# A two-block transformer kernel: the mixer's opening loads and products reordered, and the linear attention written in three tied steps per head and direction

## The chip, the core and the metric

The kernel runs on one core of one Trainium2 chip. The metric is the device time of one execution in microseconds (us). TensorE (PE) multiplies, VectorE (DVE) and ScalarE (ACT) work on tiles, GpSimd (POOL) helps, and SP issues most DMA transfers. SBUF is the memory on the core, PSUM the one into which TensorE writes.

## The reference

A first block (a mixer, then 32 experts of which four are used per token) is followed by a second block of two layers. The change lies in the mixer: it normalises 256 tokens `x` and 256 context tokens, modulates them, projects them with one wide `w_in`, runs a gated delta rule (8 heads) and a gated linear attention (GLA, 4 heads), each in both directions over context and tokens, and merges the branches.

```python
mod_lat = split(silu(c) @ w_mod + b_mod, 6); mod_ctx = split(silu(c_ctx) @ w_mod + b_mod, 6)
h_lat = rms_norm(x, norm_mix_g) * (1 + sc1) + sh1
h_ctx = rms_norm(ctx, norm_mix_g) * (1 + csc1) + csh1
p_lat, p_ctx = h_lat @ w_in, h_ctx @ w_in
# delta rule on silu(conv(q, k, v)), then the linear attention, per direction:
log_a = log_sigmoid(lr @ gla_gate_w + gla_gate_b) / 16
def step(s, xs):                       # chunks of the sequence
    intra, qg, kd, v, gl = xs          # qg = q exp(gcum), kd = k exp(gcum[-1] - gcum)
    o = intra + qg @ s                 # intra = tril((q e^(gcum-ref)) (k e^(ref-gcum))^T) v
    s = s * gl[:, None] + kd.T @ v
    return s, o
y = sigmoid(g_a) * (rms_norm(o_a) * silu(z) @ w_out_a) + sigmoid(g_b) * (rms_norm(o_b) * silu(r) @ w_out_b)
x = x + g1 * (y @ w_out)
x = x + g2 * moe_ffn(modulate(rms_norm(x)))    # 32 experts, top 4
out = second_block(x)
```

## The kernel before, in words

The program is recorded engine by engine with a tile layer: a scheduler sorts the instructions of each engine by the priority in which they were written and by its model of the engines; tiles come from pools with a tag and a number of buffers, and the layer adds the waits. So the order on an engine is not that of the code; it is shown below where it matters. Products of full accuracy are made of three: a weight `w` is split into a high part `wh` (a cast by ScalarE, line 150) and a low part `wl` (a subtraction by VectorE, line 151), and `mm3` (line 164) adds `wh`xhigh, `wh`xlow and `wl`xhigh, 24 products for the 8 rows of 128 of the inner dimension. `proj_fm` and `proj_tm` are the two forms of a projection: `proj_fm` loads 128 columns of a weight with `load_w` (line 172), splits them with `parts`, and multiplies.

`phase1` is the mixer. Its opening (lines 257 to 335) loads `x` into `xin`, eight 1 MB pieces of `w_mod` (line 250) and, between the third and the fourth, the context; then the small weights `wsm` (the gates' columns) and constants: `cum` (into `resB`), `adt` (decay rates), `cw` (convolution), `gw` (GLA gates) and a mask. `mod_mm` (line 255) multiplies a piece by the two conditioning columns `cT`. Each pair of token tiles, `x` first, is squared and scaled (lines 301 to 306), transposed on TensorE (line 311) and copied to `xT` (line 313). The modulation rows are evacuated (line 316) and transposed into columns `mc` and `G1` (lines 319 to 324). Then, for each of 8 blocks `kk`, ScalarE writes the modulated block rounded, `hTh` (line 329, two halves of 256), VectorE writes it in full, `hf` (line 331, two halves), and subtracts: `hTl` (line 333). The first products on these are the gating one, `psm` (24 products with `wsh` and `wsl`), and the first projection (columns 4640), with which the gating product shares the tag of its PSUM tile; projections of columns 1024 and 1152 follow for the convolutions, which VectorE does.

`DELTA_ORDER` is a string that sets in which order the pieces of the delta rule are written. `GLA_ORDER` does so for the linear attention and what fills it up: D (`gla_gates` for both directions of a head), O (`outputs` of a head), S, G, R, b (projections of gates and branches), v (values), B (the second branch's columns). `gla_gates` makes a gate product (line 807), a chain of exponentials on ScalarE and products on VectorE up to `qk` (line 835) and `kd`, transposes `kd` on TensorE (line 855), copies it to `kdt` (line 857), makes scores from `qk` (lines 862 and 863), a first state (line 868, copied on line 869) and a second one (line 871, scaled and added on line 872). `outputs` multiplies `qs` by the states (line 947) and the scores by the values (line 948). In the trace `pu` is the tile of the state products, `gs` that of the states.

After `phase1` the experts' weights come in transfers of 1 MB (line 1103) into buffers that free themselves as TensorE finishes with them; the second block follows.

## Time and profile before

| what | value |
|---|---|
| three runs | 2461.91, 2469.0, 2471.72 us; median 2469.0 |
| profiled execution | 2463.59 us, span on the core 2461.8 us |
| mean granted TensorE clock | 0.969 of full |
| busy: TensorE, VectorE, ScalarE, GpSimd | 2277.9, 1244.0, 925.4, 150.9 us |
| DMA | 605.87 MB, mean 246 GB/s |
| in the chain that ended last | PE 34%, DMA 10%, DVE 4% |

Busy times are sums over the whole span and say nothing of a single stage; the stages are read from windows. A wait is put down to the instruction that came last before the waiting one could start. A TensorE record's length is modelled, and neighbours overlap: the distance between starts is the pace. A float32 product that isn't split leaves two records, a product of split parts one.

### The profile page before, as it was taken

How to read it: one execution, taken by the hardware profiler on the slowest of the kernel's cores; microseconds unless marked ns; L12 is line 12 of the kernel's file. 1: busy time of each engine (PE TensorE's matmuls, PEld its weight loads, DVE VectorE, ACT ScalarE, POOL GpSimd, SP SyncE). 2: the span in 40 equal slices, each digit the busy share in tenths (PEclk: the TensorE clock that was granted, in tenths of full speed). 3: DMA queues.
4: the chain of work that ended last, by engine and by line, in shares of the span. 5: the costliest groups of instructions: out<-in, count | busy, mean ns of one | idle time of the engine just before them, and what ended most of it. 6: DMA issues, size and time to landing. Idle time of an engine off the chain costs nothing.

```text
span 2461.8 us, 36281 instructions
## 1 busy us (share of the span) xinstructions
PE 2277.9 (93%) x14402; PEld 1546.1 (63%) x14403; DVE 1244.0 (51%) x2676; ACT 925.4 (38%) x1956; POOL 150.9 (6%) x186
## 2 busy tenths in 40 slices
PE   6789878999989999999899999998999999999998
PEld 3466556889983433333334333334877999887998
DVE  4898887587561111112211111114867556867655
ACT  4556546577441101010101010103475545465545
POOL 0122122000010000000000000000011001011001
PEclk8889988999999999999999999999999999999999
DMA  8522431134897999999999999996525555534563
GB/s 288 141 79 57 121 116 35 47 92 122 260 333 307 419 420 419 420 419 420 391 419 419 421 418 420 419 420 232 149 79 156 183 172 159 155 98 141 188 188 104
DMA packets 273963, 605.87 MB, mean 246 GB/s; under 512 B 26038, under 2 KB 218681, under 8 KB 221564
## 3 DMA queue, kind: packets, MB, share of 16 engines
q1 hardware_dynamic: 266852, 595.24, 65.7%
q10 hardware_dynamic: 6280, 7.80, 1.2%
q8 instruction: 115, 1.88, 0.3%
q14 instruction: 60, 0.49, 0.1%
q0 software_dynamic: 656, 0.46, 0.1%
HBM read 602.30 MB, written 1.15 MB: 245 GB/s over the span
## 4 chain that ended last, share of the span: by engine, by line
PE 34%; DMA 10%; DVE 4%; issue 2%; ACT 1%; POOL 0%; ACTq 0%; SPq 0%; DVEq 0%; POOLq 0%
PE qm L164 23%; DMA w<-in_w_gu_dram 7%; PE yd L1376 2%; DMA w<-in_w_down_dram 2%; PE gt L1360 2%; PE lt L1360 1%; PE qm L1814 1%; DVE wl L151 1%; PE tr L1345 1%; DVE u L1620 0%; DVE ul L151 0%; PE tr L1289 0%; PE qp L1881 0%; ACT wh L150 0%; PE lt L1365 0%
## 5 line engine op out<-in xcount | busy, mean ns | idle before, releaser
L150 ACT CAST wh<-w 128x1024 fp32r<-128x1024 f32 (+2 forms) x318 | 318.5, 1002 | 285.4 <-PE qm L164 203.6
L151 DVE TENSOR_TENSOR wl<-w,wh 128x1024 fp32r<-128x1024 f32 (+2 forms) x318 | 371.4, 1169 | 39.9 <-ACT wh L150 38.2
L1253 ACT ACTIVATE sg<-g 128x1024 f32<-128x1024 f32 x16 | 16.9, 1057 | 720.4 <-DVE g L1251 720.4
L164 PE MATMUL qm<-uh,wh 128*128 128x272 f32 (+2 forms) x1008 | 261.8, 294 | 0.5 <-ACT wh L150 0.3
L164 PE MATMUL qm<-ul,wh 128*128 128x272 f32 (+2 forms) x1008 | 258.4, 289 | 1.2 <-DVE ul L151 1.2
L1251 DVE TENSOR_SCALAR g<-gt 128x1024 f32<-128x1024 f32 x16 | 19.6, 1225 | 462.9 <-PE gt L1365 407.3
L1376 PE MATMUL yd<-w,aT 128*64 128x512 f32 x1024 | 228.6, 601 | 0.0
L164 PEld LDWEIGHTS qm<-uh,wh 128*128 128x128 f32 (+1 forms) x1008 | 189.2, 188 | 10.2 <-issue 5.8
L164 PEld LDWEIGHTS qm<-ul,wh 128*128 128x128 f32 (+1 forms) x1008 | 189.9, 189 | 3.1 <-DVE ul L151 1.6
L1360 PE MATMUL lt<-w,resB 128*64 128x512 f32 x512 | 187.9, 593 | 0.6 <-DVE act L1252 0.6
L1360 PE MATMUL gt<-w,resB 128*64 128x512 f32 x512 | 183.0, 600 | 4.8 <-DMA w<-in_w_gu_dram 4.8
L1360 PE MATMUL lt<-w,xg 128*64 128x512 f32 x512 | 185.3, 593 | 0.0
L1360 PE MATMUL gt<-w,xg 128*64 128x512 f32 x512 | 175.3, 597 | 8.6 <-DMA w<-in_w_gu_dram 8.5
L1376 PEld LDWEIGHTS yd<-w,aT 128*64 128x64 f32 x1024 | 73.0, 139 | 142.6 <-issue 139.8
L1275 DVE TENSOR_TENSOR ys<-yd,g2r 128x512 f32<-128x512 f32 x32 | 20.6, 686 | 249.5 <-PE yd L1376 233.0
L164 PE MATMUL qm<-uh,wl 128*128 128x272 f32 (+2 forms) x1008 | 145.4, 286 | 0.0
L164 PE MATMUL mm<-hTh,wh 128*128 128x256 f32 (+1 forms) x384 | 130.1, 358 | 8.5 <-ACT wh L150 4.1
L164 PEld LDWEIGHTS qm<-uh,wl 128*128 128x128 f32 (+1 forms) x1008 | 132.6, 188 | 0.5 <-issue 0.4
L164 PE MATMUL qm<-fl,wh 128*128 128x272 f32 (+1 forms) x512 | 128.5, 286 | 0.0
L164 PE MATMUL qm<-fh,wh 128*128 128x272 f32 (+1 forms) x512 | 127.3, 286 | 0.0
L164 PE MATMUL mm<-hTl,wh 128*128 128x256 f32 (+1 forms) x384 | 125.9, 347 | 0.0
L1360 PEld LDWEIGHTS lt<-w,resB 128*64 128x64 f32 x512 | 57.7, 137 | 74.1 <-issue 72.1
(586 smaller groups left out, 4349.3 us busy)
## 6 DMA issues: line engine op xcount, KB each, us to landing
w<-in_w_gu_dram SPq DMA_DIRECT2D x256, 1024.0 KB
w<-in_w_down_dram SPq DMA_DIRECT2D x128, 1024.0 KB
w<-in_w_ff_dram SPq DMA_DIRECT2D x64, 1024.0 KB
w<-in_w_in_dram SPq DMA_DIRECT2D x72, 512.0 KB
w<-in_w_in_dram SPq DMA_DIRECT2D x30, 1024.0 KB
y<-in_w_mod_dram SPq DMA_DIRECT2D x19, 1024.0 KB
w<-in_w_out_dram SPq DMA_DIRECT2D x24, 512.0 KB
w<-in_w_mod_dram SPq DMA_DIRECT2D x5, 1024.0 KB
```

The costliest lines, as they stand in the source:

```text
L150: k.nc.scalar.copy(hi, x)
L151: k.nc.vector.tensor_sub(lo, x, hi.bitcast(F32))
L164: mm = nc.tensor.matmul(out, l, r, start=start and n == 1, stop=stop and n == 3 * len(terms))
L1251: nc.vector.tensor_scalar(g, gt, 7.0, LOW / 1.702, op0=ALU.min, op1=ALU.max)
L1253: nc.scalar.activation(sg, g, AF.Exp, scale=-1.702)
L1275: nc.vector.tensor_mul(ys[:, js], yd[:, js], g2r[:, js])
L1345: nc.tensor.matmul(o, hx[:, t, f * 128:(f + 1) * 128], S[t].rearrange("p e s -> p (e s)"), start=(t == 0 and i == 0), stop=(t == 1 and i = ...
L1360: nc.tensor.matmul(quarter(j)[64 * i:64 * i + 64], xg[:, kk, c0:c0 + CAP], w[i][:, j * 512:(j + 1) * 512], start=(kk == 0), stop=False)
L1376: nc.tensor.matmul(yd[64 * i:64 * i + 64, j * 512:(j + 1) * 512], aT[:, 2 * f2 + f, 64 * i:64 * i + 64], w[i][:, f, j * 512:(j + 1) * 512] ...
L1814: nc.tensor.matmul(o[r, f:], v[:n, j, r], keys(ts[i], j, n)[:, f - KQ[j]:], start=(j == 0), stop=(j == 2))
```

## The change

Opening: the context's load is issued right behind that of `x`; the weights of the first three projections (columns 4640, 1024, 1152) are loaded right behind the small weights, ahead of the constants, and kept in `first`; the products of `mod_mm` are written behind all transposes, and normalisation and transposes have a loop each; the splits of the first two weights are written ahead of the `hTh` loop; in that loop ScalarE now writes `hf` in full, VectorE casts it to `hTh` (one step of 512) and subtracts; `psm` takes its PSUM tile from the small products' buffers.

Linear attention: `gla_gates` is a generator of three steps, d (gate product and chain), e (transposes of `kd` and scores), f (states), named by letters of their own in `GLA_ORDER`. Steps d, e, f, the outputs O and the branches' columns C and B are written under `tc.issue_after`, which adds an ordering edge, without a semaphore, from the last product of the latest projection to each of their TensorE instructions. `qs` moves to another tag with five buffers.

```diff
@@ -188,7 +188,8 @@
 DELTA_ORDER = "EkPPKPKPKPKMmXXXXXXXXXPQPQPVVHHkqSSSSSSSSPPQPQPVVHHSSSSSSSSEkPPKPKPKPKMXXXXXXXXXPQPQPVmVHHSSSSSSSSkPPQPQPVqqVHHSSSSSSSSqvv"
 
 
-GLA_ORDER = "DSGGGGOvDSGODGSORvDSRGRBBBGbORbbBbbbbb"
+
+GLA_ORDER = "dsdGCefdGGGGefOdvefdsGCefOdvefdsGCefOdRsefGCRBefORBBbRbbBbbbbb"
 
 
 def phase1(k, A, B):
@@ -257,12 +258,13 @@
 
     xin = pro.tile([128, 4, 1024], F32, name="xin")
     nc.sync.dma_start(xin[:, 2:4, :], a["x"][0].rearrange("(t p) d -> p t d", p=128))
+    nc.sync.dma_start(xin[:, 0:2, :], a["ctx"][0].rearrange("(t p) d -> p t d", p=128))
     wm = [mod_piece(big([2048]), kk, 0) for kk in range(3)]
-    nc.sync.dma_start(xin[:, 0:2, :], a["ctx"][0].rearrange("(t p) d -> p t d", p=128))
     wm += [mod_piece(pro.tile([128, 2048], F32, name=k.nm("w"), tag="w", bufs=5), kk, 0) for kk in range(3, 8)]
     wsm = pro.tile([128, 8, 64], F32, name="wsm")
     nc.sync.dma_start(wsm[:, :, 0:32], w_in[:, 7200:7232].rearrange("(k p) c -> p k c", p=128))
     nc.sync.dma_start(wsm[:, :, 32:64], w_in[:, 4096:4128].rearrange("(k p) c -> p k c", p=128))
+    first = {c: load_w(k, w_in[:, c:c + 128]) for c in (4640, 1024, 1152)}
     co = CONST_OFF["cum"][0]
     nc.sync.dma_start(B[:, 1024:1408], a["cst"][:, co:co + 384])
     cum, blk64 = B[:, 1024:1280], B[:, 1280:1408]
@@ -287,9 +289,6 @@
     nc.vector.tensor_scalar_add(cT, cT, 1.0)
     nc.vector.reciprocal(cT, cT)
     nc.vector.tensor_mul(cT, cT, vecT[:, 0:16])
-    mp = smps()
-    for kk in range(8):
-        mod_mm(mp, wm[kk], kk, 2)
 
 
     ss = pro.tile([128, 4], F32, name="ss")
@@ -304,6 +303,7 @@
         rsqrt_small(k, pro, rstd[:, 2 * p:2 * p + 2], v, 2)
         for t in (2 * p, 2 * p + 1):
             nc.vector.tensor_scalar_mul(xin[:, t, :], xin[:, t, :], rstd[:, t:t + 1])
+    for p in (1, 0):
         for kk in range(0, 8, 2):
             pt = mmps()
             for i in range(2):
@@ -311,6 +311,9 @@
                     nc.tensor.transpose(pt[:, i * 256 + t * 128:i * 256 + (t + 1) * 128],
                                         xin[:, 2 * p + t, (kk + i) * 128:(kk + i + 1) * 128], ident)
             nc.scalar.copy(xT[:, kk:kk + 2, 256 * p:256 * p + 256], pt.rearrange("p (i c) -> p i c", i=2))
+    mp = smps()
+    for kk in range(8):
+        mod_mm(mp, wm[kk], kk, 2)
     m1 = A[0:2, 0:2048]
     for j in range(4):
         (nc.scalar.copy if j % 2 else nc.vector.tensor_copy)(m1[:, j * 512:(j + 1) * 512], mp[32 * j:32 * j + 2, :])
@@ -323,23 +326,25 @@
     G1 = pro.tile([128, 2, 8], F32, name="G1")
     nc.vector.scalar_tensor_tensor(G1, mc[:, :, 8:16], 1.0, vecT[:, 16:24].unsqueeze(1).to_broadcast([128, 2, 8]),
                                    op0=ALU.add, op1=ALU.mult)
+    for c in (4640, 1024):
+        first[c] = parts(k, first[c])
     for kk in range(8):
         hf = pro.tile([128, 512], F32, name=k.nm("hf"), tag="hf", bufs=3)
         for r, cs in ((1, slice(0, 256)), (0, slice(256, 512))):
-            nc.scalar.activation(hTh[:, kk, cs], xT[:, kk, cs], AF.Identity, scale=G1[:, r, kk:kk + 1],
-                                 bias=mc[:, r, kk:kk + 1])
-            nc.vector.tensor_scalar(hf[:, cs], xT[:, kk, cs], G1[:, r, kk:kk + 1], mc[:, r, kk:kk + 1],
-                                    op0=ALU.mult, op1=ALU.add)
+            nc.scalar.activation(hf[:, cs], xT[:, kk, cs], AF.Identity, scale=G1[:, r, kk:kk + 1], bias=mc[:, r, kk:kk + 1])
+        nc.vector.tensor_copy(hTh[:, kk, :], hf)
         nc.vector.tensor_sub(hTl[:, kk, :], hf, hTh[:, kk, :].bitcast(F32))
+
+    made_by = [None]
 
     def at(x, i):
         return x[i] if isinstance(x, Halves) else x[:, i, :]
 
-    def proj_fm(src, xh, xl):
-
-        wh, wl = parts(k, load_w(k, src))
+    def proj_fm(src, xh, xl, w=None):
+
+        wh, wl = w if isinstance(w, tuple) else parts(k, load_w(k, src) if w is None else w)
         o = mmps(xh.shape[-1])
-        mm3(nc, o, [(wh[:, kk, :], wl[:, kk, :], at(xh, kk), at(xl, kk), True) for kk in range(8)], True, True)
+        made_by[0] = mm3(nc, o, [(wh[:, kk, :], wl[:, kk, :], at(xh, kk), at(xl, kk), True) for kk in range(8)], True, True)
         return o
 
     def proj_tm(src, tiles, xh, xl, evac):
@@ -351,8 +356,8 @@
                 if half == 0:
                     os_[i] = ps.tile([128, 256], F32, name=k.nm("tm"), tag=("mm", "sm")[i // 2], bufs=2)
                 ts = slice(t * 128, (t + 1) * 128)
-                mm3(nc, os_[i], [(wh[:, kk, :], wl[:, kk, :], at(xh, 4 * half + kk)[:, ts], at(xl, 4 * half + kk)[:, ts], False)
-                                 for kk in range(4)], half == 0, half == 1)
+                made_by[0] = mm3(nc, os_[i], [(wh[:, kk, :], wl[:, kk, :], at(xh, 4 * half + kk)[:, ts],
+                                               at(xl, 4 * half + kk)[:, ts], False) for kk in range(4)], half == 0, half == 1)
         for i, t in enumerate(tiles):
             evac(t, os_[i])
 
@@ -368,7 +373,7 @@
     for kk in range(8):
         nc.scalar.copy(v4(wsh)[:, kk, :, 0:16], w4[:, kk])
         nc.vector.tensor_sub(v4(wsl)[:, kk, :, 0:16], w4[:, kk], v4(wsh)[:, kk, :, 0:16].bitcast(F32))
-    psm = mmps()
+    psm = smps()
     mm3(nc, psm, [(wsh[:, kk, :], wsl[:, kk, :], hTh[:, kk, :], hTl[:, kk, :], True) for kk in range(8)], True, True)
     lr = one.tile([48, 512], F32, name="lr")
     ba = B[0:48, 0:512]
@@ -477,7 +482,7 @@
 
         if ct in ahead:
             return ahead.pop(ct)
-        return proj_fm(w_in[:, ct * 128:ct * 128 + 128], *((lat_h, lat_l) if ct < 8 else (hTh, hTl)))
+        return proj_fm(w_in[:, ct * 128:ct * 128 + 128], *((lat_h, lat_l) if ct < 8 else (hTh, hTl)), first.pop(ct * 128, None))
 
     def conv_silu(ct):
         o, lat_only = conv_cols(ct), ct < 8
@@ -526,7 +531,7 @@
     gk = [A[:, 512 * h:512 * h + 512] for h in range(4)]
 
     def fill_gk(h):
-        nc.scalar.copy(gk[h], proj_fm(w_in[:, 4640 + h * 128:4768 + h * 128], hTh, hTl))
+        nc.scalar.copy(gk[h], proj_fm(w_in[:, 4640 + h * 128:4768 + h * 128], hTh, hTl, first.pop(4640 + h * 128, None)))
 
     def fill_gq(h):
         t = wd.tile([128, 256], F32, name=k.nm("gq"), tag="gq", bufs=4)
@@ -839,7 +844,7 @@
         nc.scalar.activation(off, off, AF.Exp, scale=0.0625)
         nc.vector.tensor_mul(off[:, 0], off[:, 0], qT.rearrange("p (t c) -> p t c", c=128)[:, :, sh])
         nc.vector.tensor_mul(off[:, 1], off[:, 1], kT[:, 256:512].rearrange("p (t c) -> p t c", c=128)[:, :, fh])
-        qs = wd.tile([128, 256], F32, name=k.nm("qs"), tag="os", bufs=2)
+        qs = wd.tile([128, 256], F32, name=k.nm("qs"), tag="kT", bufs=5)
         nc.scalar.activation(qs, G[:, 256:512], AF.Exp, scale=0.0625)
         nc.vector.tensor_mul(qs, qs, qT)
         glt = wd.tile([128, 1], F32, name=k.nm("glt"), tag="glt", bufs=2)
@@ -850,6 +855,7 @@
         nc.scalar.activation(kd, kd, AF.Exp, scale=0.0625)
         nc.vector.tensor_mul(kd[:, 0:256], kd[:, 0:256], kT[:, 0:256])
         nc.vector.tensor_mul(kd[:, 256:384], kd[:, 256:384], kT[:, 256 + fi * 128:384 + fi * 128])
+        yield
         pk = smps(384)
         for t in range(3):
             nc.tensor.transpose(pk[:, t * 128:(t + 1) * 128], kd[:, t * 128:(t + 1) * 128], ident)
@@ -862,6 +868,7 @@
             nc.tensor.matmul(pa, ke[:, t * 128:(t + 1) * 128], qe[:, t * 128:(t + 1) * 128], start=True, stop=True)
             nc.tensor.matmul(pa[fh, sh], off[:, 1, t, :], off[:, 0, t, :], start=True, stop=True)
             nc.vector.copy_predicated(AT[:, t, :], m_gla[:, 128 * d:128 * d + 128], pa)
+        yield
         ss_ = wd.tile([128, 2, 256], F32, name=k.nm("gs"), tag="vb", bufs=2)
         p0 = ps.tile([128, 256], F32, name=k.nm("pu"), tag="pu", bufs=1)
         for t in range(2):
@@ -870,7 +877,7 @@
         p1 = ps.tile([128, 256], F32, name=k.nm("pu"), tag="pu", bufs=1)
         nc.tensor.matmul(p1, kdt[:, 2, :], gv[h][:, 2 + fi, :], start=True, stop=True)
         nc.vector.scalar_tensor_tensor(ss_[:, 1, :], ss_[:, 0, :], glt, p1, op0=ALU.mult, op1=ALU.add)
-        return qs, AT, ss_
+        yield qs, AT, ss_
 
     def silu_cols(c0, dst, ccs=range(4)):
 
@@ -948,28 +955,41 @@
                 nc.tensor.matmul(po, AT[:, t, :], gv[h][:, 2 + t, :], start=False, stop=(d == 1))
             nc.scalar.copy(ob[:, t, h, :], po)
 
+    def pinned(c, i):
+        if c in "def":
+            h, d = divmod(i, 2)
+            if c == "d":
+                two.setdefault(h, []).append(gla_gates(h, d))
+                next(two[h][d])
+            else:
+                x = next(two[h][d])
+                if c == "f":
+                    two[h][d] = x
+        elif c == "O":
+            outputs(i)
+        elif c == "C":
+            ba_.columns(i)
+        else:
+            if not bb:
+                bb.append(Branch(ob, 4, rr2, 33, big([8, 256], F32R), big([8, 256], F32R)))
+            bb[0].rms(i, 1)
+            bb[0].columns(i)
+
     for c in GLA_ORDER:
         i = count.setdefault(c, 0)
         count[c] += 1
-        if c == "D":
-            two[i] = [gla_gates(i, d) for d in range(2)]
-        elif c == "O":
-            outputs(i)
-        elif c == "S":
+        if c in "defOCB":
+            with tc.issue_after(made_by[0].ins):
+                pinned(c, i)
+        elif c == "s":
             ba_.rms(2 * i, 2)
             silu_cols(3072, z, (i,))
-            ba_.columns(i)
         elif c == "G":
             gate_cols(7232, ga, (i,))
         elif c == "v":
             fill_gv(i + 2)
         elif c == "R":
             silu_cols(6176, rr2, (i,))
-        elif c == "B":
-            if not bb:
-                bb = [Branch(ob, 4, rr2, 33, big([8, 256], F32R), big([8, 256], F32R))]
-            bb[0].rms(i, 1)
-            bb[0].columns(i)
         else:
             gate_cols(8256, gb_, (i,))
     bb = bb[0]
```

**SP's queue behind the second small weight** (`wsm`; `w` are projection weights, `resB` is `cum`). Before:

```order
L265 DMA wsm_126<-in_w_in_dram 128x8x32
L267 DMA resB_66<-in_cst_dram 128x384
L271 DMA adt_130<-in_a_log_f_dram 128x8
L271 DMA adt_130<-in_a_log_b_dram 128x8
L271 DMA adt_130<-in_dt_bias_f_dram 128x8
L271 DMA adt_130<-in_dt_bias_b_dram 128x8
L273 DMA cw_135<-in_conv_w_dram 108x2x128
L275 DMA gw_137<-in_gla_gate_w_f_dram 16x512
L276 DMA gw_137<-in_gla_gate_w_b_dram 16x512
L95 DMA cst_11_140<-in_cst_dram 128x384
L172 DMA w_47_489<-in_w_in_dram 128x8x128
L172 DMA w_51_521<-in_w_in_dram 128x8x128
```

Of the change:

```order
L266 DMA wsm_126<-in_w_in_dram 128x8x32
L172 DMA w_11_129<-in_w_in_dram 128x8x128
L172 DMA w_12_131<-in_w_in_dram 128x8x128
L172 DMA w_13_133<-in_w_in_dram 128x8x128
L269 DMA resB_66<-in_cst_dram 128x384
L273 DMA adt_136<-in_a_log_f_dram 128x8
```

Three projection weights moved ahead of nine constants.

**VectorE at the start of the `hTh` loop.** Before:

```order
L321 TENSOR_TENSOR mc_285<-sm_31_268,vecT_144 128x32
L324 SCALAR_TENSOR_TENSOR G1_287<-mc_285,vecT_144 128x16
L331 TENSOR_SCALAR hf_32_289<-xT_187,G1_287,mc_285 128x256 x2
L331 TENSOR_SCALAR hf_33_295<-xT_187,G1_287,mc_285 128x256 x2
L333 TENSOR_TENSOR hTl_94<-hf_32_289,hTh_93 128x512
L331 TENSOR_SCALAR hf_34_301<-xT_187,G1_287,mc_285 128x256
L333 TENSOR_TENSOR hTl_94<-hf_33_295,hTh_93 128x512
```

Of the change (line 335 is the cast, 336 the subtraction):

```order
L324 TENSOR_TENSOR mc_291<-sm_34_274,vecT_150 128x32
L327 SCALAR_TENSOR_TENSOR G1_293<-mc_291,vecT_150 128x16
L151 TENSOR_TENSOR wl_36_296<-w_11_129,wh_35_295 128x1024
L151 TENSOR_TENSOR wl_38_300<-w_12_131,wh_37_299 128x1024
L335 CAST hTh_93<-hf_39_303 128x512
L335 CAST hTh_93<-hf_40_308 128x512
L336 TENSOR_TENSOR hTl_94<-hf_39_303,hTh_93 128x512
L336 TENSOR_TENSOR hTl_94<-hf_40_308,hTh_93 128x512
L335 CAST hTh_93<-hf_41_313 128x512
```

The full-precision steps are gone, the casts are there, and two `wl` splits that stood at the loop's end stand ahead of the first cast.

**TensorE at the last direction of the last head in the linear attention.** Before (855 transposes of `kd`, 868 and 871 the state products):

```order
L164 MATMUL tm_1096_6122<-wh_1093_6105,hTh_93 128x256
L855 MATMUL sm_1067_5975<-cst_1_61,kd_1066_5969 128x128 x3
L164 MATMUL tm_1096_6122<-wh_1093_6105,hTl_94 128x256
L164 MATMUL tm_1096_6122<-wh_1093_6105,hTh_93 128x256
L164 MATMUL tm_1096_6122<-wh_1093_6105,hTl_94 128x256
L164 MATMUL tm_1096_6122<-wh_1093_6105,hTh_93 128x256
L164 MATMUL tm_1096_6122<-wh_1093_6105,hTl_94 128x256
L868 MATMUL pu_1073_5992<-gv_1028_5760,kdt_1068_5979 128x256 x2
L164 MATMUL tm_1095_6109<-wl_1094_6106,hTh_93 128x256 x4
L164 MATMUL tm_1096_6122<-wl_1094_6106,hTh_93 128x256 x2
L871 MATMUL pu_1074_5996<-gv_1028_5760,kdt_1068_5979 128x256
```

Of the change (861 transposes, 875 and 878 state products, 931 transposes of a branch's columns, 954 and 955 outputs):

```order
L931 MATMUL sm_1111_6235<-cst_1_61,yt_1110_6232 128x128
L861 MATMUL sm_1112_6244<-cst_1_61,kd_1052_5898 128x128 x3
L931 MATMUL sm_1111_6235<-cst_1_61,yt_1110_6232 128x128 x3
L875 MATMUL pu_1118_6261<-gv_983_5514,kdt_1113_6248 128x256 x2
L878 MATMUL pu_1119_6265<-gv_983_5514,kdt_1113_6248 128x256
L954 MATMUL mm_1121_6274<-gs_1117_6260,qs_1050_5893 128x256
L955 MATMUL mm_1121_6274<-gv_983_5514,AT_1114_6250 128x256
L954 MATMUL mm_1120_6268<-gs_1117_6260,qs_1050_5893 128x256
L955 MATMUL mm_1120_6268<-gv_983_5514,AT_1114_6250 128x256
```

The transposes, the state products and the outputs stand closer together, and the projection products between them are gone.

## Rows read from the trace of the kernel before

**Rows 1.** Waits of the DMA queue on SP, 600 to 800 us; total, times, longest

```profile
SPq L1103 <- PE lt L1360: 33.9, 13, 18.1
```

**Rows 2.** Windows; start:end, length, busy time by engine, granted clock, DMA share, GB/s

```profile
30.30:37.20 6.90, 4.52 (x42) 1.81 (x40) 3.04 (x13) 3.22 (x14) 0.00 (x0) 0.99 0.69 177
37.20:47.40 10.20, 8.75 (x16) 4.41 (x17) 9.99 (x24) 9.68 (x18) 0.00 (x0) 0.50 0.83 287
80.00:100.00 20.00, 13.76 (x164) 7.22 (x162) 19.25 (x39) 13.67 (x23) 3.38 (x5) 0.83 0.41 159
419.50:433.10 13.60, 8.79 (x91) 7.76 (x92) 11.44 (x15) 5.59 (x23) 8.33 (x7) 0.50 0.01 1
433.10:474.00 40.90, 40.90 (x295) 32.16 (x294) 18.96 (x56) 17.56 (x57) 0.62 (x2) 1.00 0.15 39
474.00:600.00 126.00, 123.22 (x870) 109.52 (x869) 102.28 (x257) 90.80 (x221) 1.87 (x6) 1.00 0.34 93
1600.00:1650.00 50.00, 47.62 (x201) 18.22 (x199) 8.89 (x12) 4.50 (x6) 0.00 (x0) 1.00 1.01 420
```

**Rows 3.** TensorE in order of time, opening; start, length, line, output and inputs, count

```profile
30.44 2.76 PE L255 MATMUL sm<-w,cT 128*2 128x512 f32 x24
38.22 0.77 PE L164 MATMUL mm<-hTh,wsh 128*128 128x512 f32 x1 [1.73 <-issue]
...
46.24 0.63 PE L164 MATMUL mm<-hTh,wh 128*128 128x512 f32 x1
46.67 0.63 PE L164 MATMUL mm<-hTl,wsh 128*128 128x512 f32 x1
...
49.33 2.03 PE L164 MATMUL mm<-hTh,wsl 128*128 128x512 f32 x8
51.20 0.39 PE L164 MATMUL mm<-hTh,wh 128*128 128x512 f32 x1
...
53.62 2.03 PE L164 MATMUL mm<-hTh,wl 128*128 128x512 f32 x8
```

**Rows 4.** DMA issues on SP in order of time, opening

```profile
13.94 10.86 SPq L265 DMA_DIRECT2D wsm<-in_w_in_dram  x1
...
33.19 2.32 SPq L172 DMA_DIRECT2D w<-in_w_in_dram  x3
```

**Rows 5.** VectorE and ScalarE in order of time, opening

```profile
36.75 0.18 DVE L324 SCALAR_TENSOR_TENSOR G<-mc,vecT 128x16 f32<-128x16 f32 x1
...
44.91 1.98 ACT L150 CAST wh<-w 128x1024 fp32r<-128x1024 f32 x2
...
46.66 1.22 DVE L151 TENSOR_TENSOR wl<-w,wh 128x1024 fp32r<-128x1024 f32 x1
47.79 0.69 DVE L333 TENSOR_TENSOR hTl<-hf,hTh 128x512 fp32r<-128x512 f32 x1
```

**Rows 6.** Instructions of line 504; durations least, median, most in ns

```profile
L504 DVE TENSOR_SCALAR acc<-acc x24: 279/426/925, 71.0 to 404.3; 128x512 f32<-128x512 f32 x16, 128x256 f32<-128x256 f32 x8
```

**Rows 7.** Waits of TensorE, 430 to 640 us

```profile
PE ch L862 <- DVE qk L835: 2.8, 6, 0.6
```

**Rows 8.** TensorE, ScalarE, VectorE in order of time, last gates of the linear attention

```profile
590.09 0.48 ACT L857 COPY kdt<-sm 128x384 f32<-128x384 f32 x1
590.62 1.13 PE L868 MATMUL pu<-gv,kdt 128*128 128x256 f32 x4
...
591.79 0.37 ACT L869 COPY gs<-pu 128x256 f32<-128x256 f32 x1
592.31 0.61 PE L871 MATMUL pu<-gv,kdt 128*128 128x256 f32 x2
...
592.96 0.48 DVE L872 SCALAR_TENSOR_TENSOR gs<-gs,glt,pu 128x256 f32<-128x256 f32 x1
```

**Rows 9.** Line 869's waiters (the copy of the first state); us, times

```profile
  PEld pu L871: 0.8, 3
```

**Rows 10.** TensorE in order of time, start of the output projection

```profile
644.54 3.64 PE L164 MATMUL mm<-hv,wh 128*128 128x256 f32 x16 [2.35 <-ACT wh L150]
```

## The prediction

> **What bounds the kernel now.** I read the page first, then the windows, then the order of time on each engine, and last the waits. The change touches only the first 640 of 2461.8 us, the mixer. What follows it is the stream of the experts' weights, at 420 GB/s with all DMA time taken, as in the stretch from 1600 to 1650 us [rows 2]. That stream waits for TensorE to free its buffers: behind the MoE's first products the queue waited 33.9 us, 18.1 of them at once [rows 1]. So a mixer that ends earlier starts the stream earlier, and I pass a gain on one to one.
>
> Inside the mixer the limit changes by stage [rows 2]. [...] From 80 to 100 us VectorE is the limit (19.25 of 20), in convolutions and decay matrices. From 433.1 us on TensorE is (40.90 of 40.90, then 123.22 of 126.00). So a gain in the opening counts if VectorE's convolutions start earlier, and one in the linear attention only if it closes an idle gap of TensorE; those sum to 126.00 - 123.22 = 2.8 us in the stretch of the gates.
>
> **The opening.** Before, twelve modulation products (24 records) ran in a lump from 30.44 to 33.20 us [rows 3], behind the context's transposes. When had their weights landed? x, the context and eight pieces are 10.5 MB, 25 us at 420 GB/s [rows 2]; with some 3 us ahead of the first byte, near 28 us, an estimate, and at the latest at 30.44, where they were used. Now the context is loaded second, its transposes go ahead of most products, and a piece's four products follow its landing. At full clock a product takes 2.76/12 = 0.23, at half 0.46: four in 1.9 us, less than the 2.5 us in which a 1 MB piece arrives. So they end near 28 + 0.8 + 1.9 = 30.7, call it 30.8, at either clock, and the modulation columns, ready at 36.75 + 0.18 = 36.9 before [rows 5], near 34.5.
>
> Not all of that arrives. The new order puts two `wl` splits ahead of the first cast on VectorE, and their `wh` among ScalarE's first steps. Before, SP's queue was held 10.86 us by the second small weight and issued the three projection weights only at 33.19 [rows 4]; now they go right behind it. At 0.52 MB each and the 287 GB/s of the stretch from 37.2 to 47.4 [rows 2] one takes 1.8 us; from 29.5 us, behind the small weights, the second lands near 33.1, an estimate. ScalarE then does `wh`, half an `hf`, `wh` (1.0 + 0.5 + 1.0, from 33.5) and VectorE the second `wl`, 1.22 [rows 5]: the first cast starts near 37.2 and the first product at 37.7 instead of 38.22 [rows 3]. How a split ahead delays is in the trace: the last `hTl`, whose inputs were there, began at 47.79, with the `wl` of 46.66 just ahead of it [rows 5]. [...] Were it otherwise, the casts could begin at 34.5 and the end below would come some 1.5 us earlier.
>
> VectorE's loop loses sixteen `hf` steps and gains eight casts. No row shows a 128x512 cast between SBUF tiles on VectorE; the nearest are a step with one source of that size, median 0.426 [rows 6], and `hTl` with two, 0.69 [rows 5]. I take 0.43, as a cast has one source: 0.43 + 0.69 = 1.1 a round, against 10.2/8 = 1.27 before. But TensorE is then the limit. From the first small product to the end of the first projection there are 48 products of 512 columns, before as now. One takes 0.43 us at half clock (46.24 to 46.67) and (51.20 - 49.33)/8 = 0.234 at full [rows 3]. If the clock returns at 47.4 as before, (47.4 - 37.7)/0.43 = 22.6 are done by then, and 25.4 x 0.234 = 5.9 plus 0.4 for the gate transposes between them follow: 53.7, against 53.62 + 2.03 = 55.6 [rows 3]. **Opening: -1.9 us.** Bounds: at full clock throughout, VectorE's pace decides, 37.2 + 8 x 1.1 = 46.0, then 22 products and the transposes, 5.5: 51.5, or -4.1. At half clock throughout, 37.7 + 48 x 0.43 + 0.4 = 58.7, or +3.1. The clock's rows favour the middle: it was low behind a thin stretch (4.52 of 6.90 us busy) and rose behind a dense one (8.75 of 10.20) [rows 2], and both stay. The constants that now load behind 1.5 MB more may hold ScalarE's exponential of the decay rates for up to 1.5 us; `hf` steps of 0.5 a half run ahead of VectorE's 1.1, so I count nothing. VectorE, full until past 100 us, carries the 1.9 on.
>
> **The delta rule between.** The scheduler shuffles it, and by the order 27 more 256-column products stand ahead of the first gate product. TensorE is full from 433.1 us [rows 2], where these lie: worth 0.
>
> **The linear attention.** Before, the score products waited for VectorE's `qk` six times, 2.8 us in all, 0.6 at most [rows 7]. At the nearest, 65 projection products now stand between gate product and use, where there were 49: 16 more of half of 0.234 are 1.9 us, more than the longest wait. So I take all: -2.8, bounds 0 and -2.8. The price is at the other end. The old order had four to eight projection products in each hop. From the transposes to the first `pu`: the copy takes 0.48 from 590.09, `pu` starts at 590.62, 0.53 together. From the first `pu` to the second: the copy takes 0.37 and the product starts 0.52 behind the copy's start (591.79 to 592.31); with about 0.4 from the product ahead to a copy that comes at once, 0.9 (an estimate). From the second to the outputs: the state step starts 0.65 behind `pu` and takes 0.48, 0.9 behind the product's own 0.25 [rows 8]. The new order leaves barer places: two of the first hop with about 0.28 of small transposes in them, 2 x 0.25 = 0.5; three of the second with two products, one, and none, 2 x 0.65 + 0.9 = 2.2; four of the third with one pair of products, 4 x 0.65 = 2.6. Of these 5.3 the trace already pays 0.8 [rows 9]: +4.5. **Linear attention: +1.7 us**, bounds -2.8 and the slower rival's below.
>
> **Sum:** -1.9 + 0 + 1.7 = -0.2 on the profiled execution's 2463.6, so 2463.4. The median shown lies 5.4 above that execution: 2468.8 us.
>
> **Rivals.** *Faster.* The opening's clock stays up (-4.1), the bare hops are covered (-2.8), the 2.35 us for which TensorE waited for `wh` ahead of the output projection go with the branch's new end [rows 10], and the stretch 419.5 to 433.1, run at half clock with 8.79 us busy [rows 2], comes out at full clock, up to 4.4: -13.7, 2455. For it: every part has its row. Against it: the edit reaches the last two only through the scheduler. *Slower.* The bare hops at full price: eight direction steps pay 0.53 + 0.9 and four outputs 0.9, 15.0 us, and ahead of every second of the sixteen copies a `wh` cast of 1.0 stands on ScalarE [rows 5], 8.0, and a `wl` of 1.22 ahead of every state step, 9.8; less 3.7 for 32 products that remain between, 0.8 paid today, and the 2.8 and 1.9 gained: +23.6, 2492.6. It needs engines that are late: ScalarE is 72% busy there (90.80 of 126.00), VectorE 81% [rows 2], and it comes out beyond noise from some two thirds of that price. Against it: the copies in [rows 8] come soon behind their products, though VectorE and ScalarE had as much to do. *The opening gains nothing:* the second weight lands 2 us later than estimated, the casts wait for its `wl`, and the first projection ends as before: +1.7, 2470.7. *The change doesn't do what it says in the linear attention:* the order shows the new places, but `qk` comes late all the same: +2.6, 2471.6.
>
> **How the numbers follow.** The forecast has 0.5, the two small rivals 0.17 together, the faster rival 0.2, the slower 0.13. Within 0.5% (12.3 us, about what a measurement of this kernel can tell from no change) lie the forecast and the small ones: 0.67. The forecast's own bounds, -4.1 - 2.8 and +3.1 + 4.5, make 2462 to 2477; the range 2453 to 2482 goes on to the faster rival and part of the way to the slower, and leaves out some 2 in 10.
>
> **What would show it.** Right: modulation columns near 34.5 us, two `wl` ahead of the first cast, half clock until about 47, the first projection's end near 53.7; no score product waiting for `qk`, and new waits of TensorE for the copies and state steps, 4 to 5 us in all. Wrong: a first projection that ends at 55.6 or later, more than 10 us of idle TensorE between 474 and 600, or a mixer that ends over 6 us earlier or later.

## The result, and the profile after

The changed kernel takes 2481.99 us, the median of five runs (2474.26 to 2484.78), against 2469.0 for the kernel before. The ratio is 1.0051, 95% interval 1.0036 to 1.0066: slower by 0.5%, outside the scatter, where the forecast said no change (2468.8). It lies just inside the range that was given, 2453 to 2482. The profiled executions lie further apart than the medians, 2483.04 against 2463.59: that of before is below its median, that of the change a little above its own. What follows looks for the 19.5 us between these two.

TensorE's first product of the experts (`gt`, line 1380 now) starts at 763.1 us instead of 742.2, and the last of the group at 1565.0 instead of 1543.9, by the list of that line's instructions (shortest, median, longest in ns, then the first and last start):

```profile
L1380 PE MATMUL gt<-w,resB x512: 592/592/1116, 763.1 to 1565.0; 128*64 128x512 f32 x171
```

So the mixer ends 21 us later, and that is passed on one to one. Next to none of it comes from ahead of the linear attention. Its first gate product (`ch`, line 807 before, 812 now) starts 3.8 us later, and the 27 products that now stand ahead of it, at 0.118 each (from 405.90 to 406.49 us in the trace of before five 128x256 products take 0.59 from start to start), are 3.2 of these:

```profile
L807 PE MATMUL ch<-lr,gw x16: 587/640/692, 474.5 to 578.6; 16*128 16x512 f32 x16
L812 PE MATMUL ch<-lr,gw x16: 587/640/692, 478.3 to 585.7; 16*128 16x512 f32 x16
```

Windows of the mixer in the changed kernel, to set against [rows 2]:

```profile
30.30:37.20 6.90, 3.31 (x30) 1.48 (x22) 4.04 (x13) 4.76 (x13) 0.00 (x0) 0.89 0.97 256
37.20:47.40 10.20, 8.31 (x28) 5.74 (x29) 9.29 (x17) 7.76 (x17) 0.00 (x0) 0.74 0.91 300
80.00:100.00 20.00, 11.46 (x142) 4.87 (x140) 17.52 (x33) 12.28 (x19) 3.13 (x5) 0.83 0.40 159
433.10:474.00 40.90, 40.90 (x294) 33.17 (x295) 18.84 (x54) 16.16 (x51) 0.00 (x0) 0.98 0.17 46
474.00:600.00 126.00, 114.35 (x763) 99.05 (x764) 92.54 (x231) 81.78 (x200) 2.49 (x8) 0.96 0.28 80
600.00:640.00 40.00, 36.01 (x268) 33.16 (x268) 24.78 (x58) 25.28 (x70) 0.00 (x0) 1.00 0.39 112
```

The opening is better than before: TensorE has 0.74 of its clock from 37.2 to 47.4 us, not 0.50. From 433.1 to 474 it is as full as before, at 0.98 of the clock. The loss is in the linear attention: from 474 to 600 us TensorE is busy for 114.35 us, not 123.22, at 0.96 of its clock, and from 600 to 640 for 36.01 of 40, where before it had 39.84:

```profile
600.00:640.00 40.00, 39.84 (x321) 38.46 (x321) 29.22 (x64) 30.19 (x80) 0.00 (x0) 1.00 0.67 192
```

More idle time is 123.22 - 114.35 + 39.84 - 36.01 = 12.7 us. In windows of 1 us the clock is 1.00 in this stretch but for two places: it is 0.51 from 496.5 to 500.0 us and 0.50 from 506.8 to 513.4, 10 us together, as 126 x 0.04/0.5 gives too. 128x256 products start 0.21 us apart there (499.00, 499.21, 499.43), not 0.118, so these 10 us cost some 5 us of work, an estimate: together 17.7. The other 3 us of the 21 are in neither sum. The low clock lies at the first long waits (2.5 us for `yt`, up to 495.69, and 3.1 for `wl`, up to 507.64):

```profile
480.00:500.00 20.00, 16.74 (x104) 13.67 (x103) 19.20 (x52) 16.87 (x45) 0.00 (x0) 0.91 0.14 39
500.00:520.00 20.00, 16.95 (x90) 14.41 (x89) 13.13 (x33) 11.49 (x28) 0.62 (x2) 0.83 0.46 131
```

And these are TensorE's waits from 430 to 640 us, the whole list (total, times, longest):

```profile
PE sm L931 <- DVE yt L926: 5.7, 3, 3.0
PE mm L164 <- DVE zx L888: 3.3, 2, 1.7
PE mm L164 <- DVE wl L151: 3.1, 1, 3.1
PE tm L164 <- DVE zx L888: 2.0, 1, 2.0
PE ch L868 <- DVE qk L840: 0.7, 1, 0.7
PE pu L878 <- ACT gs L876: 0.5, 1, 0.5
PE pu L875 <- ACT kdt L863: 0.2, 1, 0.2
```

The wait for `qk` of [rows 7] fell from 2.8 to 0.7 us. In the bare hops that the prediction priced at 4.5 TensorE's products wait for 0.7 us (the last two lines). The weight loads ahead of these products, the measure of [rows 9], wait for 3.4:

```profile
  PEld pu L878: 2.3, 5
  PEld pu L875: 1.1, 3
```

Before, it was 0.8 and 0.2. In the trace these waits lie beside products that run, so they can't be added to the idle time; whether they make the 3 us that are missing above isn't shown. Seven other waits, 14.1 us together, have come: for `yt` (columns of a branch), `zx` (evacuation of a silu projection, that is, its copy out of PSUM) and `wl`. All of them end with VectorE, and the prediction's sum has none of them.

### The profile page after: what moved, and what is told of

It is laid out like the page before. It is cut to its first block, busy times and chain, and to the rows that moved or that the text cites. A ratio compares the mean times of both kernels' runs of the same rounds, so it can differ in the third digit from the quotient of the medians.

```text
span 2481.3 us, 36249 instructions
## 1 busy us (share of the span) xinstructions
PE 2284.5 (92%) x14402; PEld 1551.2 (63%) x14403; DVE 1241.4 (50%) x2668; ACT 926.2 (37%) x1956; POOL 150.3 (6%) x186
## 4 chain that ended last, share of the span: by engine, by line
PE 35%; DMA 8%; DVE 4%; issue 2%; ACT 1%; POOL 0%; ACTq 0%; SPq 0%; DVEq 0%; POOLq 0%
PE qm L164 23%; DMA w<-in_w_gu_dram 6%; PE yd L1396 3%; PE gt L1380 2%; DMA w<-in_w_down_dram 2%; PE lt L1380 2%; PE qm L1834 1%; DVE wl L151 1%; PE tr L1365 1%; DVE u L1640 0%; PE tr L1309 0%; DVE ul L151 0%; PE lt L1385 0%; PE gt L1385 0%; PE qp L1901 0%
## 5 line engine op out<-in xcount | busy, mean ns | idle before, releaser
L164 PEld LDWEIGHTS qm<-uh,wh 128*128 128x128 f32 (+1 forms) x1008 | 189.5, 188 | 10.2 <-issue 5.8
L164 PE MATMUL mm<-hTh,wh 128*128 128x256 f32 (+1 forms) x384 | 130.3, 358 | 12.7 <-ACT wh L150 4.1
```

The costliest lines, as they stand in the source:

```text
L164: mm = nc.tensor.matmul(out, l, r, start=start and n == 1, stop=stop and n == 3 * len(terms))
```

## The experiments

Each kernel was timed against the kernel before on the same chip; the chips differ from run to run, so ratios are compared, not medians. A trace shows one execution: that of e9 is the fastest of its twelve (2452.51 us), that of e3 the slowest of its eleven (2470.51). "Tie" is an ordering edge of `tc.issue_after`. In the expectations, theory A places the loss in the new linear attention (A1: by its ties; A2: by the place of the gate chain on VectorE), theory B in what the opening does to the delta rule.

| run | opening | order string | ties | median us | ratio to before (95%) |
|---|---|---|---|---|---|
| the change | new | new | all | 2481.99 | 1.0051 (1.0036 to 1.0066) |
| e1_open | new | old | - | 2474.04 | 1.0032 (1.0018 to 1.0045) |
| e2_gla | old | new | all | 2481.28 | 1.0069 (1.0055 to 1.0083) |
| e3_nopin | new | new | none | 2465.65 | 1.0003 (0.9993 to 1.0012) |
| e4_pin_def | new | new | d, e, f | 2481.22 | 1.0054 (1.0036 to 1.0072) |
| e5_pin_ocb | new | new | O, C, B | 2469.24 | 1.0015 (1.0001 to 1.0029) |
| e6_late_d | new | d later | all | 2477.84 | 1.0056 (1.0038 to 1.0074) |
| e7_gla_nopin | old | new | none | 2472.04 | 1.0018 (1.0005 to 1.0030) |
| e9_shift | new | C, B later | none | 2461.73 | 0.9979 (0.9969 to 0.9990) |
| e10_zx_act | new | new | all, `zx` on ScalarE | 2477.31 | 1.0049 (1.0031 to 1.0068) |
| e11_tie_shift | new | C, B later | all | 2469.53 | 1.0012 (1.0000 to 1.0023) |
| e12_shift_open0 | old | C, B later | none | 2468.11 | 1.0013 (1.0002 to 1.0024) |
| e13_shift2 | new | C, B later, d early | none | 2462.6 | 0.9983 (0.9970 to 0.9997) |
| e14_tie_e | new | new | e | 2485.33 | 1.0076 (1.0056 to 1.0097) |
| e15_tie_d | new | new | d | 2471.68 | 1.0026 (1.0011 to 1.0040) |
| e18_b_late | new | B later | none | 2462.72 | 0.9987 (0.9974 to 1.0000) |

### One half at a time

**Opening alone**: `gla_gates`, `GLA_ORDER` and their loop as before.

> Opening of the change, linear attention of before (its order, its undivided gate step, its tag of qs). Theory A (the whole loss comes from the linear attention's new order): 2466 to 2470 us, as before or up to 3 us faster, the delta rule's first matrix transpose near 104.7 instead of 105.85, last state product of the linear attention within 3 us of 592.9. Theory B (the opening costs through what it shuffles in the delta rule): 2474 us or more.

1.0032, about 7.8 us slower. That is the time of theory B (2474 or more), but not its place: the first gate product starts at 477.6 us, no later than in the change. The loss is in the linear attention, whose code is that of before. Its longest line of waits and a window:

```profile
PE ch L867 <- DVE qk L840: 6.0, 6, 3.4
```

```profile
540.00:560.00 20.00, 19.27 (x93) 14.62 (x94) 14.18 (x41) 11.56 (x27) 0.31 (x1) 0.77 0.13 36
```

The scheduler, starting from other times, set it in another order: between the gate product at 530.4 us and its scores at 539.9 no product of a projection stands, where before there were 45 or more each time. TensorE waits 6.0 us for `qk` instead of 2.8, once 3.4 us, and behind that wait the clock is 0.77 over 20 us, where it was 0.98 in the 20 before (at 0.50, as in the change, that would be 9.2 us, an estimate). Bare hops add 2.5 us of waits.

**Linear attention alone**: the opening of before, steps, ties and order string of the change.

> Opening of before, linear attention of the change with its ties. Theory A: 2480 us or more, TensorE 10 to 18 us behind the kernel before by 640 us, with waits of 1.5 to 3 us for zx, yt and wl on VectorE. Theory B: 2466 to 2472 us.

1.0069: the new linear attention loses with the old opening too, as theory A said.

### The ties

**No ties.**

```diff
-            with tc.issue_after(made_by[0].ins):
-                pinned(c, i)
+            pinned(c, i)
```

> The change with the new order string and the divided gate step, without any ordering edge. Theory A1 (the ties hold work back until VectorE is late): at least half of the loss goes, 2475 us or less, the two waits for yt (2.5 and 3.0 us) shrink. Theory A2 (where the gate chain stands on VectorE is what counts, the ties do little): 2479 us or more, and the three waits for zx stay.

1.0003: the whole loss is gone, and A1 holds as to the time. But its detail was wrong: the waits for `yt` stayed (5.9 us), while those for `zx` and `wl` went. The longest and the `zx` line of its list:

```profile
PE sm L931 <- DVE yt L926: 5.9, 4, 3.0
...
PE tm L164 <- DVE zx L888: 0.2, 1, 0.2
```

**The order string with d later** ("ds" to "sd", "dR" to "Rd"; all ties).

> The change with each gate step d written behind the projection next to it (ds becomes sd, dR becomes Rd), ties kept. Theory A2 (the unbroken gate chain ahead of zx on VectorE holds the PSUM tiles): the three waits of TensorE for zx (5.3 us in all) go and the time falls to 2471 to 2476 us. Theory A1: 2479 us or more. Bare hops as the price (the rival of the prediction): no change either, since the hops stay as bare.

1.0056, not to be told from the change, and the median, 2477.84, lies in neither band. The waits for `zx` went, as A2 said, but others came (2.5 us for a `y`, 1.1 for ScalarE), so the time decides nothing about A2.

**Ties on some steps**: `if c in "def":` ahead of the `with`, and `if c in "OCB":`.

> The change with its ordering edges on the steps d, e and f alone; columns and outputs are free. On TensorE the order of the linear attention stays that of the change. If the ties of d, e and f carry the loss: as the change, 0.4 to 0.7% above the kernel before (2476 to 2484 us), with the waits for zx and wl. If those of the columns and outputs do: 2464 to 2470 us.

> The change with its ordering edges on the columns C, B and the outputs O alone; d, e and f are free. If the ties of d, e and f carry the loss: as without any tie, within 0.2% of the kernel before. If those of columns and outputs do: 0.4% or more above it.

1.0054 and 1.0015: the ties on d, e and f carry the loss. Those on outputs and columns cost little or nothing.

**No ties, opening of before.**

> Opening of before, linear attention with the new order string and the divided gate step, no ties. If the ties alone make the loss of the linear attention (2481.3 with them): back to within 0.2% of before, 2462 to 2470 us. If the new order string does too: 2473 us or more.

1.0018, within the 0.2% expected, though the median, 2472.04, lies between the two bands: without ties the linear attention alone is near before. With e2, e3 and the change this makes a square: ties cost 0.51% with the old opening (1.0069 less 1.0018) and 0.48% with the new, 12 us; the new opening gains 0.18% with ties and 0.15% without, 4 us, but in both of these pairs the intervals overlap, so that gain isn't shown.

**Ties on one step** (`if c in "e":`, `if c in "d":`).

> The change with its ordering edges on step e alone (the scores). On TensorE the linear attention then stands in the order of the full change, since the scores and the next gate product share three PSUM tiles and the held scores hold the gate product 24 projection products back. If that is the whole cause: 0.4 to 0.6% above the kernel before, with the three waits for zx of 1.7, 1.7 and 2.0 us. If several ties are needed: 0.2% or less.

> Ordering edges on step d alone; the scores run as early as without ties, but the gate product stands behind the outputs, later still than in the change. If the late gate product is what costs (its chain on VectorE meets the evacuations of the next projection): 0.3% or more above the kernel before, with waits for zx or qk of 1.5 us and more. If the held scores themselves cost: within 0.2%.

The tie on the scores alone does all of it (1.0076), and its waits for `yt`, `zx` and `wl` are those of the change to a tenth of a us. That on the gate product, which puts it still later, costs 0.23% (1.0026 against 1.0003 without ties, with intervals that just touch), so my reading that a late gate product is the cause was mostly wrong. The traces show what is. In the changed kernel, TensorE at the end of a silu projection:

```profile
540.77 0.63 PE L164 MATMUL tm<-wl,hTh 128*128 128x256 f32 x4
543.08 0.36 PE L164 MATMUL mm<-hTh,wh 128*128 128x256 f32 x1 [1.68 <-DVE zx L888]
```

VectorE meanwhile, the gate chain of a second direction from its first step to the last, and `zx` behind it (eleven rows left out stand between 538.07 and 542.32 without a gap of note):

```profile
534.02 0.75 DVE L815 TENSOR_SCALAR z<-ch,vecT 128x512 f32<-128x512 f32 x1 [0.30 <-PE ch L812]
...
538.07 1.32 DVE L823 TENSOR_TENSOR_SCAN G<-ones,z 128x256 f32<-128x256 f32 x3
...
542.32 0.28 DVE L857 TENSOR_TENSOR kd<-kd,resA 128x128 f32<-128x128 f32 x1
542.52 0.74 DVE L888 TENSOR_SCALAR zx<-tm 128x256 f32<-128x256 f32 x2
```

TensorE's next product needs the PSUM tile that `zx` empties. `zx` stands behind the chain, fourteen more rows from its first step on, and comes at 542.52. TensorE, done at 541.4, waits 1.68 us. The same place without ties:

```profile
532.85 0.63 PE L164 MATMUL tm<-wl,hTh 128*128 128x256 f32 x4
533.32 0.38 PE L868 MATMUL ch<-qk 128*128 128x128 f32 x2
533.64 0.33 PE L869 MATMUL ch<-off 128*64 128x64 f32 x2
533.89 0.49 PE L868 MATMUL ch<-qk 128*128 128x128 f32 x2
534.31 0.33 PE L869 MATMUL ch<-off 128*64 128x64 f32 x2
534.57 1.12 PE L812 MATMUL ch<-lr,gw 16*128 16x512 f32 x2
535.62 0.39 PE L164 MATMUL mm<-hTh,wh 128*128 128x256 f32 x1
```

Here the other direction's scores (lines 868 and 869) and the next gate product stand between the two projections, 2.3 us of TensorE's time, and `zx` is there when they end. The chain and its collision are the same in both kernels (`zx` starts 1.1 us behind the projection's end in either); the scores and the gate product were the cover. The tie holds each score behind the last product of the latest projection, so it moves them 24 products on, the gate product comes behind them, and the cover is gone. The run with only d tied confirms the size: its scores stay and its gate product leaves, and the wait is what is then uncovered:

```profile
534.58 0.33 PE L869 MATMUL ch<-off 128*64 128x64 f32 x2
535.41 0.36 PE L164 MATMUL mm<-hTh,wh 128*128 128x256 f32 x1 [0.51 <-DVE zx L888]
```

0.51 us, against 1.68 less the scores' 1.25 (533.32 to 534.57), 0.43.

The wait for `wl` comes another way. In the changed kernel the split stands behind the last step of a chain:

```profile
506.38 2.35 DVE L151 TENSOR_TENSOR wl<-w,wh 128x1024 fp32r<-128x1024 f32 x2
```

```profile
507.64 0.58 PE L164 MATMUL mm<-hTh,wl 128*128 128x256 f32 x1 [3.05 <-DVE wl L151]
```

Without ties it stands in the middle of the chain (between steps at 503.98 and 505.31), ready for its product at 505.44:

```profile
504.18 1.21 DVE L151 TENSOR_TENSOR wl<-w,wh 128x1024 fp32r<-128x1024 f32 x1
```

So the ties also changed VectorE's own order. In the trace, 763.1 against 750.9 us at the experts' first product, the ties cost 12.2 us; waits for `zx` make 5.1 of it and for `wl` 3.1. The clock makes none, by an estimate at 0.50 for the low stretches: they take some 10 us between 474 and 640 in either (0.96 of the clock over 126 us; without ties 0.99 over 126 and 0.91 over 40). Where the rest goes isn't shown.

**`zx` taken off VectorE** (all ties; the clamp is left out).

```diff
-                nc.vector.tensor_scalar_max(x, o, LOW)
+                nc.scalar.copy(x, o)
```

> The change with all its ties, but the evacuation zx of the silu projections is done by ScalarE as a plain copy (the clamp of line 888 is left out). If zx waits because it stands behind the unbroken gate chain on VectorE: the three waits for zx (5.3 us) go, no new wait of that size stands at those places, and the time falls by 4 to 8 us against the change, to about 2474 to 2478. If the products wait for another reason: waits of the same size for the same PSUM tiles from ScalarE, and no gain.

```profile
PE mm L164 <- DVE wl L151: 4.3, 2, 2.9
...
PE ch L868 <- DVE qk L840: 2.5, 1, 2.5
PE mm L164 <- ACT zx L888: 1.5, 2, 0.7
```

Of the 5.3 us for `zx` 1.5 are left, now ScalarE's, so its place on VectorE did hold it. But the time is 1.0049, not clearly below the change: the scheduler set the start of the linear attention anew, and waits for `wl` (4.3 us) and `qk` (2.5) took the place. As a test of what these waits cost in all it is inconclusive.

### The order string

**First C ahead of the second gate step, first B behind the third output, no ties.**

```diff
-GLA_ORDER = "dsdGCefdGGGGefOdvefdsGCefOdvefdsGCefOdRsefGCRBefORBBbRbbBbbbbb"
+GLA_ORDER = "dsGCdefdGGGGefOdvefdsGCefOdvefdsGCefOdRsefGCRefOBRBBbRbbBbbbbb"
```

> No ties, opening of the change, and in the order string the first C moved ahead of the second gate step and the first B behind the third output, so that the columns stand behind more work. If waits for yt are what is left (2.5 and 3.0 us, each followed by half clock): 3 to 8 us less than without ties alone, 2457 to 2463. If not: as without ties, 2465 to 2468.

0.9979: faster than the kernel before by 4 to 5 us, and than the change by 0.7%. In its trace TensorE is nearly full again:

```profile
474.00:600.00 126.00, 123.10 (x855) 109.80 (x855) 101.08 (x255) 88.90 (x222) 1.92 (x6) 0.97 0.33 96
600.00:640.00 40.00, 38.99 (x312) 37.32 (x311) 27.81 (x65) 27.79 (x73) 0.00 (x0) 1.00 0.60 176
```

**The first B alone.**

> No ties, and in the order string the first B alone moved behind the third output; the rest as in the change. If the wait for yt near 603 us (2.99) with the half clock behind it is what the shifted run got rid of: 3 to 6 us less than without ties, 2460 to 2463, and TensorE loses some 6 us less between 600 and 640. If it is the first C that counted: as without ties, near 2465.7.

0.9987, 2462.7 us: by these values most of what the string gives is B's, though the intervals of this run, of e9 and of the run without ties overlap or nearly do. In the run without ties a wait of 2.99 us for `yt` at 603 us is followed by a low clock:

```profile
600.00:620.00 20.00, 16.36 (x89) 13.44 (x89) 7.53 (x18) 8.11 (x22) 0.00 (x0) 0.83 0.18 53
```

With B later that wait is gone. The change has it too, 3.00 us.

**Both ends, with ties, with the opening of before, and another string** ("dsdGGCefdGGGef", then as e9).

> The order string of the shifted run (0.9979 of before without ties), now with all ties. If the ties by themselves cost some 10 us whatever the string: 2470 to 2478 us, with the waits for zx back. If they only hurt the string of the change: within 0.2% of the shifted run, about 2462.

> Opening of before, linear attention with the shifted string and no ties. If the change's opening is worth what its first projection gains (2 to 3 us): 2 to 5 us above the shifted run, 2464 to 2467. If it is worth nothing by the end of the mixer: as the shifted run.

> As the shifted run (no ties, opening of the change), but the second gate step stays early and two G projections stand ahead of the first C, so that both directions' scores come later. If the wait of 2.4 us for qk that the shifted run has left is worth its own length and the half clock behind it: 2 to 5 us faster than the shifted run. If not: equal to it.

Ties on the shifted string: 1.0012, 0.33% or 8 us above it, with the waits for `zx` (5.3 us) back and none for `wl`. This pair is the nearest to a price of the waits for `zx`. The old opening with it: 1.0013, so the new one is worth 0.34%, 8 us, more than expected, and the one pair in which its gain is clear of the intervals. The second string: 0.9983, no better. Its wait for `qk` is 0.65 us, but a `y` costs 2.7 at the same time.

## Why the prediction was wrong

**The opening, -1.9 us.** Right in sign; the start was later than I said and the clock better. VectorE's start of the loop and TensorE's first and last products on it:

```profile
35.54 0.17 DVE L327 SCALAR_TENSOR_TENSOR G<-mc,vecT 128x16 f32<-128x16 f32 x1
35.80 1.23 DVE L151 TENSOR_TENSOR wl<-w,wh 128x1024 fp32r<-128x1024 f32 x1
37.38 1.22 DVE L151 TENSOR_TENSOR wl<-w,wh 128x1024 fp32r<-128x1024 f32 x1 [0.35 <-ACT wh L150]
38.52 0.77 DVE L335 CAST hTh<-hf 128x512 fp32r<-128x512 f32 x2
```

```profile
39.09 0.77 PE L164 MATMUL sm<-hTh,wsh 128*128 128x512 f32 x1 [3.81 <-DVE hTh L335]
...
50.88 2.03 PE L164 MATMUL mm<-hTh,wl 128*128 128x512 f32 x8
```

The two `wl` do stand ahead of the first cast, and a cast takes 0.42 (0.77 for two). The columns are ready at 35.7, not 34.5, the first cast comes at 38.5, not 37.2, and the first product at 39.09, later than before [rows 3]. But the clock did not stay low until 47.4: its mean there is 0.74. The first projection ends at 50.88 + 2.03 = 52.9, 2.7 us earlier than before, where I had 1.9. "VectorE carries the 1.9 on" was wrong: by the transpose of the first matrices, 105.85 us before by that trace, 1.2 us are left, since VectorE now waits for ScalarE ahead of them, where from 80 to 100 us it had been busy for 19.25 of 20:

```profile
95.40 0.69 DVE L521 TENSOR_TENSOR kT<-e,e 128x512 f32<-128x512 f32 x1 [1.83 <-ACT e L520]
...
104.66 1.98 DVE L626 STREAM_TRANSPOSE Ms<-E 128x1024 f32<-128x1024 f32 x1
```

By the first gate product nothing is left: it comes 0.6 us late, once the 27 products are taken off. So this term, carried to the end of the mixer, was wrong too. That the opening is worth 8 us with the shifted string, and costs as much with the old linear attention, is then a matter of the order behind it, and I leave the shares open.

**The delta rule, 0.** The level at its end bears this out: TensorE is full from 433.1 to 474 in both, and those 0.6 us are all that both terms together left.

**The linear attention, +1.7 us.** This is the step that failed. -2.8 for `qk` came out as -2.1. +4.5 for bare hops came out as 0.7 us of waits of the products. The 0.8 that I took off as paid already is a wait of weight loads; by that measure the hops went from 1.0 to 3.4, part of it or all under products that ran. What the sum put at nothing is the 14.1 us for `yt`, `zx` and `wl` and some 5 us of half clock. I counted which products the old order had put into the hops of the gates, and never asked the reverse: what the gates' scores covered where they stood. With the gate products they covered VectorE's chain at the end of each silu projection. I had the chain's neighbours at hand (VectorE 81% busy there) and read them as no obstacle. The rest of the 14.1 are columns and a split that came behind a chain: 3.1 for `wl`, where VectorE's own order changed, and 5.7 for `yt`. The `yt` part belongs to the order string, since it stays without ties; that string without ties takes 1.0003 with the new opening and 1.0018 with the old.

**The rivals.** The slower one had the right sign and the wrong mechanism: its price came from the hops, which held TensorE's products for 0.7 us. It said that lateness of VectorE and ScalarE would decide, and VectorE's did, at tiles it didn't name. The range reached up to 2482 on that rival's account alone, so it is luck that the measured time lies inside. The faster one lost on its first condition, a clock that stays up. e9, without the ties, gets 0.21%, some 5 of its 13.7 us. Two of the signs named for a wrong forecast came: 126.00 - 114.35 = 11.7 us of idle TensorE between 474 and 600, and a mixer that ends 21 us later.

**One to one** held: 20.9 us at the experts' first product, 21.1 at the last, 19.5 at the end.

## What to carry to other kernels

Here an ordering edge that made a burst compact also took it away from where it filled a wait (1.68 us for `zx`): before tying an instruction down, look at what stands on the other engines while it runs in its old place, above all a chain ahead of a short evacuation on which the next PSUM tile hangs, as VectorE's chain ahead of `zx`, which started 1.1 us behind its projection's end. Where a scheduler sets the order, time a change of one stage with the other stages' order held or shown: here an opening whose first projection ends 2.7 us earlier made the kernel 0.3% slower with the old linear attention, which the scheduler had reordered. Before adding edges, try moving a consumer that waits behind one more independent piece of work, as the first B here (0.9987 against 1.0003, with intervals that overlap).

## What the runs showed of the hardware

With some long waits of TensorE in a stretch that was otherwise full came a low granted clock: 3.4 us and 0.77 over 20 us (e1), 2.99 us and 0.83 (the run without ties), 2.5 and 3.05 us with 0.91 and 0.83 in the change, there 0.51 from 496.5 to 500.0 us and 0.50 from 506.8 to 513.4. It isn't a rule: behind the change's 3.00 us near 617 us the clock stayed at 1.00 to 640. In the opening the granted clock from 37.2 to 47.4 us is 0.74, with TensorE busy for 8.31 of the 10.2 us, where it was 0.50 before; what brought it back wasn't tried by itself.
